# Tying weight sums, and the first addition to h, behind earlier work on VectorE

## The chip, the cores and the metric

One core of a Trainium2 chip runs the whole program. The metric is the device time of one execution in microseconds (us). TensorE (PE) multiplies; its weight loads are a row of their own (PEld). VectorE (DVE), ScalarE (ACT) and GpSimd (POOL) do the elementwise work, and the queue of SyncE (SP) issues nearly all transfers (DMA).

## The reference

A layer of a streaming encoder on x of 512 rows by 1024 columns in float32:

```python
xn = rmsnorm(h, norm_mix_g[l])
u = jnp.einsum('bsd,de->bse', xn, w_in[l])
q, k, v, xr, gr, ga, gb = jnp.split(u, splits, axis=-1)
ya = chunked_band_attention(q, k, v, rel_table[l]) @ w_attn_out[l]
xc = causal_depthwise_conv(xr, conv_w[l], conv_b[l])
hr = rg_lru(xc, w_rg_r[l], b_rg_r[l], w_rg_i[l], b_rg_i[l], rg_lambda[l])
yb = (hr * jax.nn.gelu(gr)) @ w_rnn_out[l]
...
h = h + (g_a * ya + g_b * yb) @ w_o[l]
hn = rmsnorm(h, norm_ffn_g[l])
gu = hn @ w_ffn_in[l]
g, up = jnp.split(gu, 2, axis=-1)
h = h + (jax.nn.silu(g) * up) @ w_ffn_out[l]
```

The change touches three of these products: the v columns of `xn @ w_in`, the product with `w_o` with its addition to h, and `hn @ w_ffn_in`.

## The kernel before

Every float32 operand is held as two parts. `split(hi, lo, src)` writes the high part on ACT (line 82) and then the low part on DVE (line 83), and `mm3` makes each product from three matmuls: high by high (line 76), high by low (line 77), low by high (line 78).

The three products that the change touches are each made by a scheme with seven smaller block products in place of eight. Its kinds have names: `w11`, `w21`, `w22` take a block of the weight as it is, and `t1` to `t4` take sums of blocks: t1 = b12 - b11, t2 = b22 - t1, t3 = t2 - b11, t4 = b21 - t2. One kind is 24 matmuls on PE, and its weights come as two halves, u = 0 and u = 1, each 128 x 2 x 512. For each half a raw block is loaded into a tile `raw` (three of them in turn, and one more in the stage of the ffn), summed if the kind asks for it, and split into a tile `whl` (four in turn, so that two kinds are there at a time).

- Attention stage: `v_weights` (line 272 is the sum for t3, 276 the sum for t4). Kinds in PE's order: w11, t1, t2, w22, t3, w21, t4.
- Stage of w_o: `kept_weights`. Here sums were made ahead and stored in DRAM. `o_add` (line 1193) adds the products `o_x`, `o_y`, `o_z` to the tiles `h`, which are loaded from x by ACT's queue (line 1162). The operands `ms` come from the tiles `za` by the additions of lines 1146 to 1148 and a split.
- Ffn: six units, fg0, fu0, fg1, fu1, fg2, fu2. fg0 takes kept sums (`kept_weights`, its kind t4 loading both parts from DRAM, line 317); the other five are made in `f_weights`: line 350 (`f_sum`) makes t1 and t2, line 366 t3, line 375 t4. Blocks are 512 columns wide, 384 in fg2 and fu2. `gated` (lines 1274, 1281, 1282) adds the products up and gates them; POOL multiplies in part of them.

The order on PE is written out by hand. The order on DVE, ACT and SP in these stages isn't: a planner takes the program as it is written, and at each point gives an engine the ready instruction of highest priority, by a model of when operands are ready. An instruction that comes late in the program can so stand early in its engine's queue. On the chip each queue runs strictly in the order it got. `tc.keep_in_program_order(ins)` ties one instruction: it must stand in its engine's queue behind the one written just before it for that engine. It adds no wait. `weights(name)` makes the weights of the kind asked for and of the next one, so the sums of a kind are written where the product before it begins. In the order of the program that means, on DVE:

- the two sums of t2 are written behind the splits of t1,
- those of t3 behind the splits of w22,
- those of a unit's w11 (they make t1) behind the two additions of `gated(unit, 0, 0, ...)` of the unit before,
- those of v's t3 behind the split of `v_s3`,
- and the first `o_add` behind the splits of the weights of o's t1.

Of the kernel before, what the change touches and what calls it, by code (L numbers as in the profile page):

```python
# [11 lines left out]
ALU = mybir.AluOpType  # L12
# [3 lines left out]
D = 1024  # L16
# [22 lines left out]
def block_kernel(ctx: ExitStack, tc: tile.TileContext, x, norm_mix_g, w_in, b_merge, rel_table,  # L39
# [3 lines left out]
    pe, dve, act, pool, sp = nc.tensor, nc.vector, nc.scalar, nc.gpsimd, nc.sync  # L43
# [24 lines left out]
    def f(ap):  # L68
        return ap.bitcast(F32)
# [10 lines left out]
    def split(hi, lo, src):  # L80

        act.activation(hi, src, AF.Copy)  # L82
        dve.tensor_sub(lo, src, f(hi))  # L83
# [159 lines left out]
    v_t1, v_t2 = [], []  # L243

    def v_raw(kind, kh, half, u):
        raw = wp.tile([P, 2, S], F32, tag="raw", bufs=3, name=f"raw_v_{kind}_{kh}{half}{u}")
        at = kh * S + u * CW
        for n, gr in enumerate(v_groups[half]):
            sp.dma_start(out=raw[:, :, n * CW:(n + 1) * CW],
                         in_=w_in[at:at + CW, C_V + gr * CW:C_V + (gr + 1) * CW].rearrange("(k p) e -> p k e", p=P))  # L250
        return raw[:]
# [10 lines left out]
    def v_weights(kind):  # L262

        hl = [wp.tile([P, 2, 2, S], F32R, tag="whl", bufs=4, name=f"whl_v_{kind}_{u}") for u in range(2)]
        for u in range(2):
            if kind == "t1":
                src = v_t1[u]
            elif kind in ("t2", "t4"):
                src = v_t2[u]
            elif kind == "t3":  # L270
                src = v_raw(kind, 0, 0, u)
                dve.tensor_sub(src, v_t2[u], src)
            else:
                src = v_raw(kind, int(kind[1]) - 1, int(kind[2]) - 1, u)
                if kind == "w21":
                    dve.tensor_sub(v_t2[u], src, v_t2[u])
            split(hl[u][:, 0], hl[u][:, 1], src)
        return lambda part, k: hl[k // 2][:, part, k % 2]

    kept_sums = {(w, n): dr.tile([2, P, D], F32, name=f"{w}_t{n}") for w, n in (("o", 1), ("o", 2), ("f", 1), ("f", 2), ("f", 3))}  # L280
    kept_parts = {(w, n): dr.tile([2, P, 2 * D], F32, name=f"{w}_hl{n}") for w, n in (("o", 3), ("o", 4), ("f", 4))}

    def kept_block(dst, w, kh, half, u):
        at = kh * S + u * CW
        sp.dma_start(out=dst, in_={"o": w_o, "f": w_ffn_in}[w][at:at + CW, half * S:half * S + S].rearrange("(k p) e -> p k e", p=P))
# [24 lines left out]
    def kept_weights(w, kind):  # L310

        if (w, kind) == ("f", "t4"):
            hl = [[sums_room.tile([P, 2, S], F32R, tag=f"t{1 + u}{part}", bufs=1, name=f"whl_f_t4_{u}{part}") for part in range(2)]
                  for u in range(2)]
            for u in range(2):
                for part in range(2):
                    sp.dma_start(out=f(hl[u][part][:]).rearrange("p k e -> p (k e)"), in_=kept_parts[w, 4][u][:, part * D:(part + 1) * D])
            return lambda part, k: hl[k // 2][part][:, k % 2]
        pl, bufs = (o_room[0], 2) if w == "o" and kind in ("w11", "t2", "t4") else (wp, 4)
        hl = [pl.tile([P, 2, 2, S], F32R, tag="whl", bufs=bufs, name=f"whl_{w}_{kind}_{u}") for u in range(2)]  # L320
        for u in range(2):
            if kind[0] == "t" and (w, int(kind[1])) in kept_parts:
                sp.dma_start(out=f(hl[u][:]).rearrange("p a k e -> p (a k e)"), in_=kept_parts[w, int(kind[1])][u])
                continue
            raw = wp.tile([P, 2, S], F32, tag="raw", bufs=3, name=f"raw_{w}_{kind}_{u}")
            if kind[0] == "w":
                kept_block(raw[:], w, int(kind[1]) - 1, int(kind[2]) - 1, u)
            else:
                sp.dma_start(out=raw[:].rearrange("p k e -> p (k e)"), in_=kept_sums[w, int(kind[1])][u])
            split(hl[u][:, 0], hl[u][:, 1], raw[:])  # L330
        return lambda part, k: hl[k // 2][:, part, k % 2]

    f_sums, f_loads, room = {}, [0], []

    def f_side(unit):
        return S if unit[2] != "2" else (DFF - 4 * S) // 2

    def f_raw(unit, kind, kh, side, u):
        wide = f_side(unit)
        f_loads[0] += 1  # L340
        pl, bufs = (room[0], 1) if f_loads[0] % 4 == 0 and room else (wp, 3)
        raw = pl.tile([P, 2, S], F32, tag="raw", bufs=bufs, name=f"raw_{unit}_{kind}_{kh}{side}{u}")
        at, col = kh * S + u * CW, "gu".index(unit[1]) * DFF + int(unit[2]) * 2 * S + side * wide
        sp.dma_start(out=raw[:, :, 0:wide], in_=w_ffn_in[at:at + CW, col:col + wide].rearrange("(k p) e -> p k e", p=P))
        return raw[:, :, 0:wide]

    def f_sum(unit, n, u, a, b):

        t = f_sums[n, u] = sums_room.tile([P, 2, S], F32, tag=f"t{n}{u}", bufs=1, name=f"t{n}_{unit}_{u}")[:, :, 0:f_side(unit)]
        return dve.tensor_sub(t, a, b)  # L350

    def f_weights(unit, kind):

        hl = [wp.tile([P, 2, 2, S], F32R, tag="whl", bufs=4, name=f"whl_{unit}_{kind}_{u}")[:, :, :, 0:f_side(unit)]
              for u in range(2)]
        for u in range(2):
            if kind in ("t1", "t4"):
                src = f_sums[1 if kind == "t1" else 2, u]
            elif kind == "t2":
                ins = f_sum(unit, 2, u, f_raw(unit, kind, 1, 1, u), f_sums[1, u])  # L360
                if u == 0:
                    tc.keep_in_program_order(ins)
                src = f_sums[2, u]
            elif kind == "t3":
                src = f_raw(unit, kind, 0, 0, u)
                ins = dve.tensor_sub(src, f_sums[2, u], src)
                if u == 0:
                    tc.keep_in_program_order(ins)
            else:
                src = f_raw(unit, kind, int(kind[1]) - 1, int(kind[2]) - 1, u)  # L370
            split(hl[u][:, 0], hl[u][:, 1], src)
            if kind == "w11":
                f_sum(unit, 1, u, f_raw(unit, kind, 0, 1, u), src)
            if kind == "w21":
                dve.tensor_sub(f_sums[2, u], src, f_sums[2, u])
        return lambda part, k: hl[k // 2][:, part, k % 2]

    def prefetch(n):
        while len(made) < min(n, len(chunks), index.get(barrier[0], len(chunks))):
            name, parts, rows, kts = chunks[len(made)]  # L380
            if name[:2] == "v_":
                made.append(v_weights(name[2:]))
                continue
            if name[:2] == "o_" or name[:3] == f_units[0]:
                made.append(kept_weights(name[0], name.split("_")[1]))
                continue
            if name[:3] in f_units:
                made.append(f_weights(*name.split("_")))
                continue
# [22 lines left out]
    def weights(name, ahead=1):  # L412
        prefetch(index[name] + 1 + ahead)
        if index[name] + 1 == len(made):
            low_parts()
        return made[index[name]]
# [44 lines left out]
    for n in range(2):  # L461
        pool.dma_start(out=vr[V_BI:V_BI + 8, (1 - n) * 64:(1 - n) * 64 + 64],
                       in_=b_rg_i.rearrange("(t two p) -> two t p", two=2, p=64)[n])
# [725 lines left out]
    def o_add(banks, half, cc, last=False):  # L1189
        for a in range(2):  # L1190
            t = 2 * half + a
            hs = ht[t][:, cc * S:(cc + 1) * S]
            dve.scalar_tensor_tensor(hs, banks[a][:], 0.5, hs, ALU.mult, ALU.add)
            if last:
                junk = tg_.tile([P, S], F32, tag="tg", name=f"hj{t}_{cc}")
                act.activation(junk[:], hs, AF.Square, accum_out=q2[t][:, cc:cc + 1])
# [10 lines left out]
    def o_last_rows(jp):  # L1207
        if jp == 4:
            o_product(ox, "t4", "x22", False)
            o_add(ox, 1, 0, True)  # L1210
            o_rows(1)

    in_order = ExitStack()
    in_order.enter_context(tc.manual_schedule(engines={mybir.EngineType.PE}))
    o_product(ox, "w11", "x11", True)
    o_add(ox, 0, 0)
    o_product(oy, "w21", "x12", True)
    o_add(oy, 0, 0, True)
    o_product(oz, "t1", "s1", True)
    o_add(oz, 1, 1)  # L1220
# [154 lines left out]
    for unit in f_units[1:]:  # L1375
        n, last = int(unit[2]), unit == f_units[-1]
# [120 lines left out]
    def bank(tag, name):  # L1497
        return ps.tile([P, S], F32, tag=tag, bufs=4 if tag == "mm" else 2, name=name)
# [6 lines left out]
    with tc.manual_schedule(engines={mybir.EngineType.PE, mybir.EngineType.DVE}):  # L1505
# [3 lines left out]
        for i in plain:  # L1509
            w = weights(f"fo0_{i}", 3)  # L1510
# [15 lines left out]
        for n, i in enumerate(paired):  # L1526
            w = weights(f"fo0_{i}", 4)
# [20 lines left out]
        for n, i in enumerate(paired):  # L1548
            w = weights(f"t12_{i}", 4)
# [8 lines left out]
        w = weights(f"fo1_{plain[-3]}", 5)  # L1558
# [33 lines left out]
        last = bank("t", "po_last")  # L1592
# [41 lines left out]
```

## Time and profile before

| | us |
|---|---|
| three runs | 860.36, 860.77, 863.06 (median 860.77) |
| the profiled execution's own time | 863.98 |
| its span, first to last instruction | 862.2 |
| PE busy in it | 844.7 |
| DVE busy | 662.3 |
| ACT busy | 519.7 |
| POOL busy | 140.9 |

In lines of the profile, `out<-in` names tiles without their numbers; the first figure of a timeline's row is the start in us from the span's start, the second its length in us, and what stands in brackets is the idle time of the engine just before it and what ended that. A row of waits gives the sum, the number and the longest. PEclk is the granted share of PE's clock.

### The profile page before, as it was taken

What the parts mean: (1) busy time and instruction counts of PE and PEld (TensorE: products, weight loads), DVE (VectorE), ACT (ScalarE), POOL (GpSimd) and SP (SyncE); (2) the same over time, 40 slices, a digit from 0 to 9 for tenths busy, and PEclk for the clock granted to TensorE, in tenths of its full rate; (3) what the DMA queues carried; (4) which work ended last, traced back from release to release, by engine and by line L of the source; (5) the groups of instructions that cost most, each with busy time, mean ns of one, the idle gap of its engine ahead of it and who ended that gap; (6) DMA issues with size and microseconds to landing.
All of it is one profiled execution on the core that took longest, in us unless ns stands there. A gap on an engine that the chain in (4) does not pass through costs nothing.

```text
span 862.2 us, 11589 instructions
## 1 busy us (share of the span) xinstructions
PE 844.7 (98%) x4114; PEld 712.7 (83%) x4114; DVE 662.3 (77%) x972; ACT 519.7 (60%) x864; POOL 140.9 (16%) x179
## 2 busy tenths in 40 slices
PE   9999999999989999999999999999999999999996
PEld 7988888888868888888888787888878999988885
DVE  5667869886979788887568577788678777798985
ACT  7595848763356688787544458653664565655434
POOL 2402031231030133333000000014002212200000
PEclk9999999999999999999999999999999999999999
DMA  8433487675634333222234873545454444426642
GB/s 284 161 114 106 149 284 268 201 265 201 203 114 146 111 98 97 89 75 73 74 110 133 326 280 129 189 153 170 145 172 137 122 141 144 166 87 200 215 135 97
DMA packets 95385, 137.17 MB, mean 159 GB/s; under 512 B 7288, under 2 KB 62160, under 8 KB 94816
## 3 DMA queue, kind: packets, MB, share of 16 engines
q1 hardware_dynamic: 93696, 132.93, 47.3%
q10 hardware_dynamic: 1232, 2.95, 0.9%
q8 instruction: 32, 0.52, 0.3%
q0 software_dynamic: 400, 0.57, 0.2%
q14 instruction: 25, 0.20, 0.1%
HBM read 122.75 MB, written 13.67 MB: 158 GB/s over the span
## 4 chain that ended last, share of the span: by engine, by line
PE 68%; DVE 13%; DMA 11%; ACT 4%; issue 4%; DVEq 0%; ACTq 0%; SPq 0%
DMA raw_fu_w<-in_w_ffn_in_dram 3%; PE po_out L76 2%; PE po_out L77 2%; PE po_out L78 2%; PE o L1084 2%; PE pT L1064 2%; DMA raw_fg_w<-in_w_ffn_in_dram 2%; PE po_ga L78 2%; PE po_ya L76 2%; PE po_ya L77 2%; PE po_ya L78 2%; PE po_ga L76 2%; PE po_ga L77 2%; DMA raw_fu_t<-in_w_ffn_in_dram 1%; PE po_xr L77 1%
## 5 line engine op out<-in xcount | busy, mean ns | idle before, releaser
L1282 POOL TENSOR_TENSOR sg<-sg,keep_fu_x 128x512 f32<-128x512 f32 (+1 forms) x10 | 18.3, 1853 | 240.4 <-DVE keep_fu_x L1281 240.4
L1053 POOL TENSOR_SCALAR p<-p,rl 128x128 f32<-128x128 f32 (+3 forms) x61 | 42.7, 718 | 15.6 <-DVE rl L1049 14.8
L1047 DVE CUSTOM_DVE_ANT_0 p<-s,bias 128x128 f32<-128x128 f32 (+1 forms) x64 | 28.6, 485 | 11.1 <-PE s L1039 8.2
L1048 ACT ACTIVATE p<-p,m 128x128 f32<-128x128 f32 (+1 forms) x64 | 35.5, 555 | 2.5 <-DVE m L1047 2.2
L76 PE MATMUL po_out<-whl_fo,act_hi 128*128 128x512 f32 (+1 forms) x80 | 30.9, 386 | 0.0
L78 PE MATMUL po_out<-whl_fo,act_lo 128*128 128x512 f32 (+1 forms) x80 | 30.7, 384 | 0.0
L77 PE MATMUL po_out<-whl_fo,act_hi 128*128 128x512 f32 (+1 forms) x80 | 30.7, 384 | 0.0
L83 DVE TENSOR_TENSOR pp<-pT,pp 128x384 fp32r<-128x384 f32 (+1 forms) x48 | 26.9, 595 | 2.0 <-ACT pp L82 1.8
L77 PE MATMUL po_xr<-xnT,whl_xr 128*128 128x512 f32 (+1 forms) x80 | 27.7, 353 | 0.0
L77 PE MATMUL po_gr<-xnT,whl_gr 128*128 128x512 f32 (+1 forms) x80 | 27.5, 347 | 0.0
L78 PE MATMUL po_gr<-xnT,whl_gr 128*128 128x512 f32 (+1 forms) x80 | 27.3, 347 | 0.0
L78 PE MATMUL po_xr<-xnT,whl_xr 128*128 128x512 f32 (+1 forms) x80 | 27.2, 346 | 0.0
L76 PE MATMUL po_gr<-xnT,whl_gr 128*128 128x512 f32 (+1 forms) x80 | 27.1, 347 | 0.0
L83 DVE TENSOR_TENSOR whl_fo<-raw_fo,whl_fo 128x1024 fp32r<-128x1024 f32 x16 | 20.7, 1303 | 8.0 <-ACT whl_fo L82 8.0
L76 PE MATMUL po_xr<-xnT,whl_xr 128*128 128x512 f32 (+1 forms) x80 | 26.3, 351 | 0.4 <-ACT xnT L611 0.4
L82 ACT ACTIVATE whl_fu_t<-t_fu 128x1024 fp32r<-128x1024 f32 (+1 forms) x18 | 17.6, 985 | 13.0 <-PE fu_x L78 8.7
L76 PE MATMUL po_k<-xnT,whl_qk 128*128 128x512 f32 x64 | 25.5, 398 | 0.0
L76 PE MATMUL po_q<-xnT,whl_qk 128*128 128x512 f32 x64 | 25.5, 398 | 0.0
L76 PE MATMUL po_ga<-xnT,whl_ga 128*128 128x512 f32 x64 | 25.5, 398 | 0.0
L1275 ACT ACTIVATE sg<-sg 128x512 f32<-128x512 f32 (+1 forms) x20 | 11.9, 596 | 22.4 <-DVE sg L1274 22.0
L76 PE MATMUL po_gb<-xnT,whl_gb 128*128 128x512 f32 x64 | 25.2, 394 | 0.0
L78 PE MATMUL po_ga<-xnT,whl_ga 128*128 128x512 f32 x64 | 25.0, 391 | 0.1
(614 smaller groups left out, 3003.3 us busy)
## 6 DMA issues: line engine op xcount, KB each, us to landing
raw_qk<-in_w_in_dram SPq DMA_DIRECT2D x32, 256.0 KB, 3.1
raw_fu_w<-in_w_ffn_in_dram SPq DMA_DIRECT2D x16, 512.0 KB, 4.3
raw_fo<-in_w_ffn_out_dram SPq DMA_DIRECT2D x16, 512.0 KB, 4.1
raw_xr<-in_w_in_dram SPq DMA_DIRECT2D x8, 512.0 KB, 5.7
raw_gr<-in_w_in_dram SPq DMA_DIRECT2D x8, 512.0 KB, 4.7
raw_ga<-in_w_in_dram SPq DMA_DIRECT2D x8, 512.0 KB, 3.9
raw_gb<-in_w_in_dram SPq DMA_DIRECT2D x8, 512.0 KB, 3.8
o_b<-in_w_o_dram SPq DMA_DIRECT2D x8, 512.0 KB, 6.3
```

The lines of the kernel that those rows point to most:

```text
L76: pe.matmul(o, sh, mh, start=start, stop=False, skip_group_check=parts)
L77: pe.matmul(o, sh, ml, start=False, stop=False, skip_group_check=parts)
L78: pe.matmul(o, sl, mh, start=False, stop=stop, skip_group_check=parts)
L82: act.activation(hi, src, AF.Copy)
L83: dve.tensor_sub(lo, src, f(hi))
L1047: dve.tensor_tensor_reduce(prob[qb][:], scs[qb][:, 0:w], bias[:, S - w:S], -1.0, 3e38, ALU.add, ALU.min, nmax[:, qb:qb + 1])
L1048: act.activation(prob[qb][:], prob[qb][:], AF.Exp, bias=nmax[:, qb:qb + 1], scale=-1.0, accum_out=lsum[:, qb:qb + 1])
L1053: eng.tensor_scalar(prob[qb][:], prob[qb][:], rl[:, qb:qb + 1], 1.0, ALU.mult, ALU.mult)
L1064: pe.transpose(pt[:, at * P:(at + 1) * P], prob[qb][:, kb * P:(kb + 1) * P], ident[:])
L1084: pe.matmul(po[:, S - n:S], st, pp[i][:, part, lo:lo + n], start=kb == 0 and part == 0, stop=kb == NT - 1 and part == 1)
L1275: ins = act.activation(o, o if keep else banks[a], AF.Silu)
L1282: (pool if keep and (unit != f_units[-1] or side) else dve).tensor_mul(o, o, keep[a] if keep else banks[a])
```

## The change

It ties more of the sums, and moves two lines of the program; no instruction is added or removed.

- v's t3: both sums are tied (none was).
- kind w11 of an ffn unit: both sums (for t1) are tied and written ahead of the split of the same half (they were untied and written behind it).
- kinds t2 and t3: both sums are tied (only u = 0 was), and both are written ahead of the two splits.
- w21: the sum for t4 is written ahead of the split, untied as before.
- fg0's t4: the first of its four loads of stored parts is tied on SP.
- the first addition to h is tied on DVE.

```diff
@@ v_weights
             elif kind == "t3":
                 src = v_raw(kind, 0, 0, u)
-                dve.tensor_sub(src, v_t2[u], src)
+                tc.keep_in_program_order(dve.tensor_sub(src, v_t2[u], src))
@@ kept_weights
             for u in range(2):
                 for part in range(2):
-                    sp.dma_start(out=..., in_=kept_parts[w, 4][u][:, part * D:(part + 1) * D])
+                    ins = sp.dma_start(out=..., in_=kept_parts[w, 4][u][:, part * D:(part + 1) * D])
+                    if u == part == 0:
+                        tc.keep_in_program_order(ins)
@@ f_weights
+        srcs = []
         for u in range(2):
             if kind in ("t1", "t4"):
                 src = f_sums[1 if kind == "t1" else 2, u]
             elif kind == "t2":
-                ins = f_sum(unit, 2, u, f_raw(unit, kind, 1, 1, u), f_sums[1, u])
-                if u == 0:
-                    tc.keep_in_program_order(ins)
+                tc.keep_in_program_order(f_sum(unit, 2, u, f_raw(unit, kind, 1, 1, u), f_sums[1, u]))
                 src = f_sums[2, u]
             elif kind == "t3":
                 src = f_raw(unit, kind, 0, 0, u)
-                ins = dve.tensor_sub(src, f_sums[2, u], src)
-                if u == 0:
-                    tc.keep_in_program_order(ins)
+                tc.keep_in_program_order(dve.tensor_sub(src, f_sums[2, u], src))
             else:
                 src = f_raw(unit, kind, int(kind[1]) - 1, int(kind[2]) - 1, u)
-            split(hl[u][:, 0], hl[u][:, 1], src)
             if kind == "w11":
-                f_sum(unit, 1, u, f_raw(unit, kind, 0, 1, u), src)
+                tc.keep_in_program_order(f_sum(unit, 1, u, f_raw(unit, kind, 0, 1, u), src))
             if kind == "w21":
                 dve.tensor_sub(f_sums[2, u], src, f_sums[2, u])
+            if kind in ("w11", "w21"):
+                split(hl[u][:, 0], hl[u][:, 1], src)
+            else:
+                srcs.append(src)
+        for u, src in enumerate(srcs):
+            split(hl[u][:, 0], hl[u][:, 1], src)
@@ o_add
-            dve.scalar_tensor_tensor(hs, banks[a][:], 0.5, hs, ALU.mult, ALU.add)
+            ins = dve.scalar_tensor_tensor(hs, banks[a][:], 0.5, hs, ALU.mult, ALU.add)
+            if half == a == cc == 0 and not last:
+                tc.keep_in_program_order(ins)
```

More of the change, by code (lines that the diff above doesn't have):

```diff
@@ L316, in kept_weights @@
                 for part in range(2):
-                    sp.dma_start(out=f(hl[u][part][:]).rearrange("p k e -> p (k e)"), in_=kept_parts[w, 4][u][:, part * D:(part + 1) * D])
+                    ins = sp.dma_start(out=f(hl[u][part][:]).rearrange("p k e -> p (k e)"), in_=kept_parts[w, 4][u][:, part * D:(part + 1) * D])
+                    if u == part == 0:
+                        tc.keep_in_program_order(ins)
             return lambda part, k: hl[k // 2][part][:, k % 2]
```

## The prediction, as made before the run

> **What bounds the kernel now.** I read the page's busy times and chain first, then PE's list of waits, then the clock by windows, then the timelines of DVE, ACT and SP around each wait.
>
> ```profile
> PE 844.7 (98%) x4114; PEld 712.7 (83%) x4114; DVE 662.3 (77%) x972; ACT 519.7 (60%) x864; POOL 140.9 (16%) x179
> PE 68%; DVE 13%; DMA 11%; ACT 4%; issue 4%; DVEq 0%; ACTq 0%; SPq 0%
> ```
>
> PE is busy 98% of the span (844.7 us), so an order on DVE can bring only what PE loses. The chain still spends 24% on DVE and DMA: there are stretches in which PE runs on weights that arrive just in time. Where they came late, PE's waits say:
>
> ```profile
> PE v_z L77 <- DVE whl_v_t L83: 3.5, 1, 3.5
> PE o_z L78 <- DVE ms L83: 1.9, 1, 1.9
> PE fu_x L77 <- DVE whl_fu_t L83: 1.6, 1, 1.6
> PE fg_x L77 <- DVE whl_fg_t L83: 1.3, 2, 0.7
> PE fg_y L77 <- DVE whl_fg_w L83: 0.4, 1, 0.4
> ```
>
> Each ends with a low part (line 83) written by DVE. They sum to 8.7 us, and two cost more than their length, as the windows show (busy times, then PEclk, DMA share, GB/s):
>
> ```profile
> 249.33:252.74 3.41, 0.54 (x2) 0.49 (x3) 3.14 (x4) 0.56 (x1) 3.29 (x3) 1.00 0.01 2
> 252.74:256.15 3.41, 3.41 (x9) 2.63 (x8) 3.31 (x4) 3.38 (x5) 0.00 (x0) 0.50 0.00 0
> 484.85:488.26 3.41, 1.55 (x7) 0.87 (x6) 3.41 (x6) 1.21 (x3) 0.00 (x0) 1.00 0.94 354
> 488.26:491.67 3.41, 3.41 (x9) 2.65 (x9) 0.97 (x2) 3.03 (x5) 0.00 (x0) 0.50 0.55 211
> 720.32:723.74 3.42, 2.33 (x13) 2.33 (x14) 3.42 (x5) 0.64 (x2) 0.00 (x0) 1.00 0.13 17
> ```
>
> After a window in which PE was busy 0.54 or 1.55 of 3.41 us, it runs 3.41 us at half clock: 3.41 x 0.5 = 1.71 us lost each time. After 2.33 us busy nothing follows. The Trainium skill ("TensorE: Matmul & The Clock Gate", Part 1) puts the fall of the clock behind an idle window of about 3.4 us. By that rule the second stall, of 1.9 us, would have cost no clock and the sum below would be 1.71 less; the trace shows that it did, and the sum goes by the trace.
>
> **Part 1: v's t3.** The timelines of ACT, DVE and PE show:
>
> ```profile
> 243.82 1.99 ACT L82 ACTIVATE whl_v_t<-v_t 128x1024 fp32r<-128x1024 f32 x2
> 245.86 0.16 DVE L1049 RECIPROCAL rl<-l 128x4 f32<-128x4 f32 x1
> 249.60 1.41 DVE L272 TENSOR_TENSOR raw_v_t<-v_t,raw_v_t 128x1024 f32<-128x1024 f32 x1 [3.58 <-DMA raw_v_t<-in_w_in_dram]
> 250.93 1.21 DVE L83 TENSOR_TENSOR whl_v_t<-v_t,whl_v_t 128x1024 fp32r<-128x1024 f32 x1
> 260.24 1.22 DVE L83 TENSOR_TENSOR v_s3l<-v_s,v_s3h 128x1024 fp32r<-128x1024 f32 x1
> 263.44 1.06 ACT L82 ACTIVATE whl_v_t<-raw_v_t 128x1024 fp32r<-128x1024 f32 x1 [0.76 <-PE v_x L78]
> 252.20 0.50 PE L77 MATMUL v_z<-whl_v_t,v_s1h 128*128 128x512 f32 x1 [3.53 <-DVE whl_v_t L83]
> ```
>
> A sum for t3, two kinds early, stands at the head of DVE's queue and waits 3.58 us for its block. Behind it stands the low part of t1, whose high part was done at 245.81. Without the sum it runs from 246.02 to 247.23; PE wants it at 252.20 - 3.53 = 248.67. So the stall goes whole: 3.53, and with it the slow window, 1.71. The sum's new place is behind v_s3l (260.24), where its block has long landed. It makes the block good for the split of 263.44 and frees no buffer, so being later delays no load: cost 0, hidden as long as it ends by 263.44 (1.98 us after 261.46, for one sum of 1.41). If not, the excess falls on a split with a whole product in hand. Gain 5.24.
>
> **Part 2: the first addition to h, and the load on SP.** One row of the chain, then the timelines of DVE, PE and SP:
>
> ```profile
> 472.73 7.88 DMA h<-in_x_dram
> 480.70 0.69 DVE L1193 SCALAR_TENSOR_TENSOR h<-o_x,h 128x512 f32<-128x512 f32 x1 [4.81 <-PE o_y L77]
> 481.31 0.41 DVE L1146 TENSOR_TENSOR za<-za,za 128x256 f32<-128x256 f32 x1
> 481.64 1.22 DVE L83 TENSOR_TENSOR whl_o_t<-raw_o_t,whl_o_t 128x1024 fp32r<-128x1024 f32 x1
> 482.78 0.42 DVE L1147 TENSOR_TENSOR za<-za,za 128x256 f32<-128x256 f32 x1
> 487.99 0.59 PE L78 MATMUL o_z<-whl_o_t,ms 128*128 128x512 f32 x1 [1.86 <-DVE ms L83]
> 471.36 0.32 SPq L317 DMA_DIRECT2D whl_f_t<-f_hl  x1
> 504.80 0.38 SPq L285 DMA_DIRECT2D raw_f_w<-in_w_ffn_in_dram  x1
> ```
>
> DVE's row names PE, but the addition began when the load of h had landed (472.73 + 7.88 = 480.61): a load is what DVE waits 4.81 us for. Tied, the addition stands behind the low part of 481.64, so at least L1146 and that low part run during the wait. They took 482.78 - 481.31 = 1.47 us: the low end, with 1.86 - 1.47 = 0.39 of the stall left. If L1147 and its successor pass too, all 1.86 goes; that is the high end. I take 1.86 less 0.2, nearer the high end, because L1147 comes earlier in the program. Either way a window of 3.41 has at least 3.41 - 0.39 = 3.02 busy, above the 2.33 that cost nothing, so 1.71 goes as well. Queued behind the addition are then the other low parts of w_o's weights, used a product later.
>
> The tie on SP moves one load of 0.5 MB from 471.36 to behind 504.80. It is wanted by fg0's third product, 25 us later. At the 354 GB/s of the window above, 0.5 MB takes 1.5 us, so h lands up to 1.5 earlier. If the three others stay where they are, perhaps nothing. Ends 0 and 1.5; I take 0, since the stall is already gone. A cost below nothing would come only by contention with loads at 506, with 20 us in hand.
>
> **Part 3: the ffn's sums.** DVE's timeline, with one row of POOL's:
>
> ```profile
> 631.27 1.23 DVE L350 TENSOR_TENSOR t_fu<-raw_fu_w,raw_fu_w 128x1024 f32<-128x1024 f32 x1 [0.89 <-DMA raw_fu_w<-in_w_ffn_in_dram]
> 632.42 1.22 DVE L83 TENSOR_TENSOR whl_fg_t<-t_fg,whl_fg_t 128x1024 fp32r<-128x1024 f32 x1
> 697.84 0.96 DVE L350 TENSOR_TENSOR t_fu<-raw_fu_w,raw_fu_w 128x768 f32<-128x768 f32 x1 [0.51 <-DMA raw_fu_w<-in_w_ffn_in_dram]
> 698.16 2.89 POOL L1371 TENSOR_TENSOR act_lo<-act,act_hi 128x1024 fp32r<-128x1024 f32 x1 [22.17 <-ACT act_hi L1370]
> 698.71 3.15 DVE L83 TENSOR_TENSOR whl_fg_w<-raw_fg_w,whl_fg_w 128x768 fp32r<-128x768 f32 x1
> 705.13 0.96 DVE L350 TENSOR_TENSOR t_fu<-raw_fu_w,raw_fu_w 128x768 f32<-128x768 f32 x1 [0.51 <-DMA raw_fu_w<-in_w_ffn_in_dram]
> 718.53 1.96 DVE L366 TENSOR_TENSOR raw_fu_t<-t_fu,raw_fu_t 128x768 f32<-128x768 f32 x1 [1.35 <-DMA raw_fu_t<-in_w_ffn_in_dram]
> 720.41 0.94 DVE L83 TENSOR_TENSOR whl_fu_t<-t_fu,whl_fu_t 128x768 fp32r<-128x768 f32 x1
> ```
>
> All four of PE's ffn stalls have one pattern: a sum for a later kind waits for its block (0.89, 0.51, 0.51, 1.35) and the low part that PE wants stands behind it. Each sum takes 1 to 2 us besides its wait, more than the stall it makes (0.7, 0.4, 0.6, 1.6). At 698.71 the low part without the sum starts near 697.3 and misses the POOL instruction that stretched it. Tied, the L350 sums stand behind the additions of `gated(0, 0)`, after t4's low parts; L366 behind w22's. So all of 3.4 goes.
>
> What it costs: a unit's w11 sums now wait for the additions at the end of the unit before. Take fu0 to fg1, in the timelines of POOL, DVE and PE and a row of the chain:
>
> ```profile
> 592.05 4.45 POOL L1282 TENSOR_TENSOR sg<-sg,keep_fu_x 128x512 f32<-128x512 f32 x2 [1.76 <-DVE keep_fu_x L1281]
> 593.62 1.71 DVE L83 TENSOR_TENSOR whl_fg_w<-raw_fg_w,whl_fg_w 128x1024 fp32r<-128x1024 f32 x1
> 595.02 0.39 PE L76 MATMUL fg_x<-whl_fg_w,hn 128*128 128x512 f32 x1
> 595.25 0.39 PE L77 MATMUL fg_x<-whl_fg_w,hn 128*128 128x512 f32 x1
> 593.13 4.08 DMA raw_fg_t<-in_w_ffn_in_dram
> ```
>
> Matmuls start 595.25 - 595.02 = 0.23 apart, so a product is 24 x 0.227 = 5.45, and t4 before it began at 589.57: the additions can end at about 589.57 + 0.2 (the last matmul's 0.39 beyond the step of 0.23) + 0.69 (the addition of 480.70, of the same shape) = 590.5. Sum, low part, sum, low part, at some 1.15 each, end at 595.1. PE wants the first low part at 595.25 (it is there at 592.8) and the second at the eighth matmul, 595.02 + 7 x 0.227 = 596.61: 1.5 in hand. One multiplication of line 1282 between costs 0.7. Beside POOL's multiplications a DVE operation took 1.71 in place of 1.2, 0.5 more; two of them cost 1.0. So at worst by rows 0.2 is missed, at each of two passages from a u unit to a g unit; 0 to 0.4 together, and I take 0.2. At the passages from g to u POOL does nothing. The next loads start when these blocks are freed, at 595.1 in place of 593.13: landed at 599.2 (4.08 later). Their two sums and two low parts, 4.6 us, end by 603.8. t2 starts two products after 595.02, at 605.9 or later: 2.1 in hand, cost 0. The sums of t2 and t3 ahead of both splits, and t4's sum ahead of w21's, put one sum (1.15) more before a low part that has some 2 in hand as well: cost 0, and 0.1 a kind if that cover goes.
>
> **The sum.** 3.53 + 1.71 + 1.86 + 1.71 + 3.4 = 12.2, less 0.2 for part 2, 0.2 for part 3, and 0.2 for a new small wait = 11.6. Against the profiled execution's 863.98: 852.4. The runs' median, 860.77, is 3.2 lower. The three runs are 860.36, 860.77 and 863.06; the step of 2.3 is near one slow window (1.71). A stall of 1.86 lies over half in one window of 3.41 only in some runs, so I take the median to lack the second slow window: 11.6 - 1.71 = 9.9, and 860.77 - 9.9 = 850.9.
>
> **The rivals.**
>
> 1. POOL takes back a part. The w11 sums now start just when POOL multiplies what the additions gave. The low part of 698.71 took 3.15 beside POOL's instruction of 698.16, where that of 720.41 took 0.94; it was held to about the other's end, which speaks for it. 1.71 for 1.2 at 593.62 speaks against. As a mechanism from rows: at each of two passages two operations are held by 2.2 (half of 4.45), and 4.4 less the 1.5 in hand is 2.9, twice: 850.9 + 5.8 = 856.7; 854 to 858.2 as a case, 0.18. The Trainium skill ("SBUF — State Buffer", the section on two separate sides) says of a DVE operation with two SBUF inputs and a GpSimd one that whichever starts first gets the shared ports for the whole instruction, the other "fully blocks". By that rule this rival's time is the forecast; 698.71 agrees with it, 593.62 does not.
> 2. The change does not do what it says: the planner, whose order shifts elsewhere, brings other sums or loads ahead of needed low parts. Only sums are tied; L375 is not, nor three of the loads on SP. Against it: PE's list holds no other wait over 0.4 us but that at the very start. Gains of 9.9 given back to within the bound: 858.2 to 863.4, middle 860.8. 0.11.
> 3. Slower: blocks freed late. With three or four raw tiles, a tied sum that holds its block holds the next load, and each of five ffn units falls behind. It decides from 9.9 / 5 = 2.0 lost in each unit, with 2.1 in hand: a delay of 4.1 a unit, one more round of a load (4.08). At 5 x 2.8 lost: 865. Against it: DVE has 98 - 77 = 21 points of the span less to do than PE. 0.09.
>
> **How the numbers follow.** Forecast 0.57: 848.1 to 854. Better, 0.05: second slow window in the median after all. About 0.3%, 2.6 us, is what a measurement here can tell from no change. Faster 0.57 + 0.05 + 0.18 = 0.80, same 0.11, slower 0.09. The low end 848.1 is all 12.2 with 0.5 for runs; the high end 859.5 takes in rival 1 and the near half of rival 2.
>
> **What would show it.** Right: PE's waits on whl_v_t and ms are gone, no window at half clock in the middle, no wait of L272 or L350 ahead of a low part in need. Part 2's low end: a wait on ms of about 0.4. Rival 1: PE waits at the second low part of w11 in fg1 and fg2. Rival 3: DVE waits on DMA at L350 for t2, with PE's waits on t2 in every unit. The prediction is wrong if PE's idle time stays near 10 us.

## The result, and the profile after

| | before | after | ratio, 95% interval |
|---|---|---|---|
| median, us | 861.91 (860.36 to 863.39, 4 runs) | 849.93 (849.69 to 850.82, 4 runs) | 0.9863 (0.984 to 0.9886) |
| profiled execution, us | 863.98, span 862.2 | 849.69, span 847.9 | |

The change makes the kernel 12.0 us faster by the medians, 14.3 by the two profiled spans. From the page of the changed kernel, its busy times and chain:

```profile
PE 839.1 (99%) x4114; PEld 710.8 (84%) x4114; DVE 663.2 (78%) x972; ACT 522.5 (62%) x864; POOL 140.6 (17%) x179
PE 82%; DVE 8%; ACT 4%; DMA 3%; issue 2%; ACTq 0%; DVEq 0%
```

The work is the same: the counts of these five engines are those of before. PE's share of the chain rose from 68 to 82%, and DMA's fell from 11 to 3%: PE runs on weights that arrive just in time in far less of the span. PE's listed waits are now these three, all in the first 25 us:

```profile
PE busy L439 <- DVE eps_t L445: 1.2, 1, 1.2
PE po_xr L76 <- ACT xnT L615: 0.4, 2, 0.2
PE pt_mix_0t L613 <- DVE xs_mix L593: 0.2, 1, 0.2
```

All five lines shown of before are gone, and so are the two windows at half clock. Two windows at the places of the two long stalls (busy times of PE, PEld, DVE, ACT, POOL, then PEclk, DMA share, GB/s):

```profile
248.41:251.82 3.41, 3.31 (x15) 2.43 (x14) 3.38 (x3) 2.98 (x5) 3.41 (x2) 1.00 0.00 0
480.00:483.41 3.41, 3.41 (x16) 2.83 (x16) 1.68 (x3) 2.57 (x4) 0.00 (x0) 1.00 0.90 330
```

DVE's timeline at v (lines of the source stand 2 to 6 further down than before):

```profile
244.51 0.16 DVE L1053 RECIPROCAL rl<-l 128x4 f32<-128x4 f32 x1
244.59 1.19 DVE L83 TENSOR_TENSOR whl_v_t<-v_t,whl_v_t 128x1024 fp32r<-128x1024 f32 x1
254.54 1.21 DVE L83 TENSOR_TENSOR v_s3l<-v_s,v_s3h 128x1024 fp32r<-128x1024 f32 x1
255.68 1.21 DVE L272 TENSOR_TENSOR raw_v_t<-v_t,raw_v_t 128x1024 f32<-128x1024 f32 x1
```

The low part of t1 follows the reciprocal at once; the sum that waited 3.58 us for its block now runs behind v_s3l, with no wait. The stall isn't gone to the last bit, though, as ACT, DVE and PE show:

```profile
245.82 1.06 ACT L82 ACTIVATE v_s4h<-v_s 128x1024 fp32r<-128x1024 f32 x1 [2.30 <-DVE whl_v_t L83]
247.86 1.42 DVE L83 TENSOR_TENSOR whl_v_t<-v_t,whl_v_t 128x1024 fp32r<-128x1024 f32 x1 [1.48 <-ACT whl_v_t L82]
249.33 0.50 PE L77 MATMUL v_z<-whl_v_t,v_s1h 128*128 128x512 f32 x1
```

Before, ACT made both high parts of t1 together (243.82, two instructions). Now the split of v_s4 stands between them in its queue and waits 2.30 us, so the second low part of t1 ends only at 247.86 + 1.42 = 249.28. PE, which issues a matmul every 0.23 us here, issued the one before at 248.84 and the one that reads this part at 249.33. With the longer step behind it that is 0.4 us, too little for the list of waits.

At o, DVE's and SP's timelines:

```profile
470.54 0.42 DVE L1151 TENSOR_TENSOR za<-za,za 128x256 f32<-128x256 f32 x1
470.89 1.22 DVE L83 TENSOR_TENSOR whl_o_t<-raw_o_t,whl_o_t 128x1024 fp32r<-128x1024 f32 x1
473.49 0.69 DVE L1197 SCALAR_TENSOR_TENSOR h<-o_x,h 128x512 f32<-128x512 f32 x1 [1.39 <-DMA h<-in_x_dram]
473.46 2.60 SPq L285 DMA_DIRECT2D raw_o_w<-in_w_o_dram  x2
```

The second sum for ms (L1147 before, L1151 now) and the low part run ahead of the first addition to h, whose wait for its load fell from 4.81 to 1.39 us. The passage from fu0 to fg1, on DVE, POOL and PE:

```profile
579.10 1.30 POOL L1288 TENSOR_TENSOR sg<-sg,keep_fu_x 128x512 f32<-128x512 f32 x1
579.76 1.72 DVE L83 TENSOR_TENSOR whl_fg_w<-raw_fg_w,whl_fg_w 128x1024 fp32r<-128x1024 f32 x1 [1.17 <-ACT whl_fg_w L82]
581.40 1.21 DVE L352 TENSOR_TENSOR t_fg<-raw_fg_w,raw_fg_w 128x1024 f32<-128x1024 f32 x1
582.54 0.68 DVE L1287 TENSOR_TENSOR keep_fu_x<-fu_y,keep_fu_x 128x512 f32<-128x512 f32 x1
583.14 1.21 DVE L352 TENSOR_TENSOR t_fg<-raw_fg_w,raw_fg_w 128x1024 f32<-128x1024 f32 x1
583.29 2.21 POOL L1288 TENSOR_TENSOR sg<-sg,keep_fu_x 128x512 f32<-128x512 f32 x1 [2.90 <-DVE keep_fu_x L1287]
584.27 2.31 DVE L83 TENSOR_TENSOR whl_fg_w<-raw_fg_w,whl_fg_w 128x1024 fp32r<-128x1024 f32 x1
585.27 0.39 PE L76 MATMUL fg_x<-whl_fg_w,hn 128*128 128x512 f32 x1
```

PE begins w11 at 585.27 and wants its second low part at the eighth matmul, 585.27 + 7 x 0.227 = 586.86. The low part ends at 584.27 + 2.31 = 586.58. So 0.3 us is in hand, and no more.

**Where 14.3 us came from.** A stall costs PE more than its listed idle: the step to the stalled matmul is longer than the usual step by the idle plus 0.16 (the modelled length of the matmul before it, 0.39, less the step of 0.23), and the step after it is 0.11 longer. That is 0.27 beside every listed wait (rows under e6). A window at half clock cost less than the 1.71 that the prediction takes, as PE's timeline of before shows:

```profile
253.22 0.63 PE L77 MATMUL v_z<-whl_v_t,v_s1h 128*128 128x512 f32 x1
253.65 0.63 PE L78 MATMUL v_z<-whl_v_t,v_s1l 128*128 128x512 f32 x1
259.16 0.39 PE L76 MATMUL v_x<-whl_v_t,v_s2h 128*128 128x512 f32 x1
```

A step at half clock is 0.43, not quite twice 0.227. From the stalled matmul of 252.20 to that of 259.16, 23 steps later, it is 6.96 us in place of 23 x 0.227 = 5.22. Of the 1.74 too much, 0.11 is the step behind the stall, so the window cost 1.6; the one at o cost 1.6 too, counted in the same way.

In the trace of before: v_z 3.53 + 0.27 = 3.80; o_z 1.86 + 0.27 = 2.13; four waits in the ffn 3.4 + 4 x 0.27 = 4.5; two windows at half clock, 3.2. Together 13.6, less the 0.4 that is left at v: 13.2. By the matmuls' starts PE in the trace of before falls another 0.9 us behind ahead of v's stall, at a wait of 0.25 (`s L1038 <- DVE m L1047`) and at smaller steps. That part isn't the change's: the profiles of e3 and e11, without v's tie, lack this wait, and that of e5, with it, has it. With it the sum is 14.1 of the 14.3.

### The profile page after: what moved, and what is told of

Its sections match the earlier page's. It is cut to its first block, busy times and chain, and to the rows that moved or that the text cites. A ratio compares the mean times of both kernels' runs of the same rounds, so it can differ in the third digit from the quotient of the medians.

```text
span 847.9 us, 11598 instructions
## 1 busy us (share of the span) xinstructions
PE 839.1 (99%) x4114; PEld 710.8 (84%) x4114; DVE 663.2 (78%) x972; ACT 522.5 (62%) x864; POOL 140.6 (17%) x179
## 4 chain that ended last, share of the span: by engine, by line
PE 82%; DVE 8%; ACT 4%; DMA 3%; issue 2%; ACTq 0%; DVEq 0%
PE fu_x L78 2%; PE fu_x L76 2%; PE fu_x L77 2%; PE po_out L76 2%; PE po_out L77 2%; PE po_out L78 2%; PE o L1088 2%; PE fg_x L78 2%; PE fg_x L76 2%; PE fg_x L77 2%; PE pT L1068 2%; PE po_ga L78 2%; PE po_ya L78 2%; PE po_ya L77 2%; PE po_ya L76 2%
## 5 line engine op out<-in xcount | busy, mean ns | idle before, releaser
L1051 DVE CUSTOM_DVE_ANT_0 p<-s,bias 128x128 f32<-128x128 f32 (+1 forms) x64 | 28.6, 485 | 11.6 <-PE s L1043 10.2
L83 DVE TENSOR_TENSOR whl_fu_w<-raw_fu_w,whl_fu_w 128x1024 fp32r<-128x1024 f32 (+1 forms) x18 | 22.1, 1227 | 8.5 <-ACT whl_fu_w L82 8.5
L83 DVE TENSOR_TENSOR whl_fu_t<-t_fu,whl_fu_t 128x1024 fp32r<-128x1024 f32 (+1 forms) x18 | 23.8, 1324 | 4.8 <-ACT whl_fu_t L82 4.6
L82 ACT ACTIVATE whl_fu_w<-raw_fu_w 128x1024 fp32r<-128x1024 f32 (+1 forms) x18 | 17.8, 989 | 13.0 <-issue 7.1
L76 PE MATMUL po_ga<-xnT,whl_ga 128*128 128x512 f32 x64 | 25.4, 397 | 0.0
```

Of the source, the lines that this page charges most:

```text
L76: pe.matmul(o, sh, mh, start=start, stop=False, skip_group_check=parts)
L1051: dve.tensor_tensor_reduce(prob[qb][:], scs[qb][:, 0:w], bias[:, S - w:S], -1.0, 3e38, ALU.add, ALU.min, nmax[:, qb:qb + 1])
```

## The experiments

Kernels e1 to e4 were timed beside runs of the kernel before with a median of 861.79 (23 runs); e5, e6, e10, e11 beside 862.31 (7); e7, e8, e9 beside 862.47 (7). Ratios are to these.

**e1, e4, e2, e3: each part alone, on the kernel before.**

e1, v's tie:

```diff
-                dve.tensor_sub(src, v_t2[u], src)
+                tc.keep_in_program_order(dve.tensor_sub(src, v_t2[u], src))
```

> The kernel before with the two sums of v's t3 tied, nothing else. Theory A (each tie takes away one stall of its own, and a stall costs PE its listed idle time, some 0.27 us around it and, where it fell, a slow window): PE's wait on whl_v_t goes (3.53), with 0.14 around it and 1.7 of half clock, so 5.4 us less, ratio 0.9937; o_z and the ffn keep their waits (1.9, 3.4 in sum). Theory B (PE, once ahead, meets the next late operand): PE's waits behind the v stage grow by what was gained, and the time falls by under 2.5 us.

856.41 us, 0.9945 (0.9928 to 0.9962): theory A. The wait of v_z is gone. The wait of o_z was shorter in this profile, 1.5 us, with this window around it:

```profile
478.41:481.82 3.41, 1.91 (x9) 1.28 (x8) 3.41 (x6) 1.06 (x3) 0.00 (x0) 1.00 1.03 410
```

No window at half clock follows: with 1.5 idle, any window of 3.41 has at least 1.9 busy.

e4, the tie on SP:

```diff
+                    if u == part == 0:
+                        tc.keep_in_program_order(ins)
```

> The kernel before with only the first load of fg0's t4 tied on SP. Theory A: no stall of PE hangs on it; 0 us, the wait on ms stays at 1.9. Theory B (the load held up the queue and the load of h): h lands 1.5 us or more earlier, the wait on ms falls to 0.4 or less and the second slow window goes: 1.5 to 3.5 us less.

861.0 us, 0.9989 (0.9975 to 1.0004): no difference that this can tell. o_z still waits, 1.1 us; it waited 1.1 in e3's profile too, which hasn't this tie, so the smaller wait is no effect of it.

e2, the tie on the first addition to h:

```diff
+            if half == a == cc == 0 and not last:
+                tc.keep_in_program_order(ins)
```

> The kernel before with only the first addition to h tied. Theory A: it runs behind one low part and L1146 to L1147 and the wait on ms is 0 to 0.4 us; 2.0 us less, and 3.7 less against those runs of before that had a second slow window. Theory B: the addition still waits for the load of h at the head of the queue and the wait on ms stays above 1 us; under 1 us less.

861.2 us, 0.9994 (0.9975 to 1.0014). The wait on ms is gone, yet the median is only 0.6 us lower. The interval reaches to 2.1 us less, so theory A's 2.0 is at its very edge. PE's waits and DVE's timeline in the ffn say where the gain went:

```profile
PE fg_x L77 <- DVE whl_fg_t L83: 2.2, 3, 1.2
PE s L1038 <- DVE m L1047: 0.7, 1, 0.7
629.79 1.23 DVE L350 TENSOR_TENSOR t_fu<-raw_fu_w,raw_fu_w 128x1024 f32<-128x1024 f32 x1 [1.10 <-DMA raw_fu_w<-in_w_ffn_in_dram]
632.20 0.50 PE L77 MATMUL fg_x<-whl_fg_t,hn 128*128 128x512 f32 x1 [1.20 <-DVE whl_fg_t L83]
```

fg_x waited 1.3 us in all before, 2.2 now. The untied sum stands ahead of the low part and waits for a load; PE comes earlier, the load not by as much, so part of the gain is given back there. The starts of the same matmuls in the two traces give the size. PE in e2 is 0.5 us behind before at the matmul ahead of o_z's stall (486.19 for 485.73), 3.3 ahead of it once the stall and the window at half clock are past (488.45 for 491.74), and 1.5 ahead at fu2's stall (719.93 for 721.41): 3.8 gained, 1.8 given back. Against an execution of before without the second window at half clock the gain at o would be 2.1, by the stall's steps, and 1.8 given back leaves little of that. (The wait of 0.7 on m lies ahead of all that this edit touches.)

e3, the sums of the ffn as changed (f_weights whole, of which this is the core):

```diff
+                tc.keep_in_program_order(dve.tensor_sub(src, f_sums[2, u], src))
...
+                tc.keep_in_program_order(f_sum(unit, 1, u, f_raw(unit, kind, 0, 1, u), src))
...
+        for u, src in enumerate(srcs):
+            split(hl[u][:, 0], hl[u][:, 1], src)
```

> The kernel before with f_weights as changed (ties on both sums of t1, t2 and t3, sums ahead of the splits), nothing else. Theory A: PE's four waits in the ffn go, 3.39 idle and 0.27 around each: 4.5 us less, ratio 0.9948. Theory B: PE comes to the ffn no earlier than before and the late part only moves: under 2 us less, with a wait of PE on the second low part of w11 in fg1 or fg2.

856.93 us, 0.9945 (0.9924 to 0.9965), as theory A has it. One wait of 0.5 is left in the ffn. The profile holds v's stall at 3.5 us as before, but more of the clock is lost behind it:

```profile
246.89:250.30 3.41, 0.87 (x4) 0.38 (x2) 1.67 (x2) 0.00 (x0) 2.88 (x5) 1.00 0.21 74
250.30:253.71 3.41, 2.50 (x6) 2.02 (x7) 3.31 (x4) 2.50 (x3) 1.33 (x1) 0.50 0.00 0
253.71:257.13 3.42, 3.42 (x10) 2.65 (x9) 2.79 (x3) 2.13 (x4) 0.00 (x0) 0.50 0.00 0
```

Two windows at half clock in place of one. The first of them begins while PE still stands (it starts again at 251.21), so it costs less than a whole one: from 251.21 to the 23rd step behind it, at 259.33, it is 8.12 us, 2.9 too much, where before has 1.74. The same stall so costs one window or two, here 1.2 us more.

The four ratios leave 4.7 + 0.9 + 0.5 + 4.7 = 10.8 us; the change brings 11.8.

**e11: the tie on h with the sums of the ffn** (the edits of e2 and e3), to see whether e2's gain comes out once the ffn gives nothing back.

```diff
+            if half == a == cc == 0 and not last:
+                tc.keep_in_program_order(ins)
...
+                tc.keep_in_program_order(f_sum(unit, 1, u, f_raw(unit, kind, 0, 1, u), src))
...
```

> The kernel before with the tie on the first addition to h and with the sums of the ffn as in the changed kernel; v's sum and SP's load stay as before. Alone, the tie on h took the wait on ms away and left the time (0.9994), and the ffn's ties alone gave 0.9945. Theory A (what the h tie gained was given back at the untied sums of the ffn, whose waits for blocks go by the loads and not by PE): with both, no wait on ms and no wait of the ffn, the time is 1.4 to 2.2 us less than with the ffn's ties alone, ratio 0.992 to 0.993 to the kernel before. Theory B (the wait on ms costs no time at all, because PE catches up behind it on something else): the same as the ffn's ties alone, ratio 0.9945.

854.59 us, 0.9905 (0.989 to 0.9919), clear of e3's interval. PE's only long wait is v's 3.5. The step from e3 is 3.4 us by the ratios, more than the 1.4 to 2.2 expected. This profile lost one window behind v and e3's two: v_z's 24 matmuls took 10.79 us here (247.70 to 258.49) and 11.96 in e3's (247.37 to 259.33), which is 1.2 of it, if the other runs were alike. So the tie on h is worth about 2 us beside the ffn's ties; alone, no gain of it shows clear of the noise.

**e6: the change without the tie on h.**

```diff
-            ins = dve.scalar_tensor_tensor(hs, banks[a][:], 0.5, hs, ALU.mult, ALU.add)
-            if half == a == cc == 0 and not last:
-                tc.keep_in_program_order(ins)
+            dve.scalar_tensor_tensor(hs, banks[a][:], 0.5, hs, ALU.mult, ALU.add)
```

> The changed kernel without the tie on the first addition to h; the tie on SP stays. Theory A (the addition stands again ahead of the first sums for ms and waits for h's load): PE has a wait on ms of 1.1 to 1.9 us, as in the kernels that had the other ties alone, and the time is 1.4 to 2.2 us (the wait and 0.27 beside it) above the changed kernel, 3.9 with a window at half clock behind it: ratio 0.988 to 0.991 to the kernel before. Theory B (the load on SP alone brings h in time, or what is gained at ms is given back later): no wait on ms, or one that does not show in the time, ratio 0.986.

852.34 us, 0.9879 (0.9864 to 0.9893): theory A, at its lower edge. DVE's and PE's timelines:

```profile
474.95 0.69 DVE L1197 SCALAR_TENSOR_TENSOR h<-o_x,h 128x512 f32<-128x512 f32 x1 [4.09 <-DMA h<-in_x_dram]
480.41 0.39 PE L76 MATMUL o_z<-whl_o_t,ms 128*128 128x512 f32 x1
480.64 0.39 PE L77 MATMUL o_z<-whl_o_t,ms 128*128 128x512 f32 x1
482.24 0.50 PE L78 MATMUL o_z<-whl_o_t,ms 128*128 128x512 f32 x1 [1.21 <-DVE ms L83]
482.58 0.40 PE L76 MATMUL o_z<-whl_o_t,ms 128*128 128x512 f32 x1
```

With the tie on SP kept, the addition still waits 4.09 us and PE 1.21. These rows also price a stall: the step to the stalled matmul is 1.60, less the usual 0.23 makes 1.37, and the next step of 0.34 adds 0.11. That is 1.48 for a listed 1.21.

**e5: the change without the tie on SP.**

```diff
-                    if u == part == 0:
-                        tc.keep_in_program_order(ins)
```

> The changed kernel without the tie on SP's load: the first of the four loads of f_hl is again issued early, as in the kernel before. Theory A (the tie on SP brings nothing by itself, because the wait on ms went with the tie on DVE, and PE has slack there): PE has no wait on ms over 0.2 us, h lands up to 1.4 us later than in the changed kernel, and the time is that of the changed kernel, ratio 0.986 (0.984 to 0.988) to the kernel before. Theory B (the tie is needed, since h's load and the raw weights of w_o share SP's queue with it): the raw_o_w loads again issue some 9 us later, behind a wait of SP on h of about 7 us, DVE waits for them in the next product and PE has a wait of over 1 us near 480 to 495, ratio 0.988 or more.

849.74 us, 0.9854 (0.9839 to 0.9868): theory A. SP's timeline of e5:

```profile
468.11 6.86 SPq L317 DMA_DIRECT2D whl_f_t<-f_hl  x3
475.07 2.23 SPq L285 DMA_DIRECT2D raw_o_w<-in_w_o_dram  x2
```

SP is held 6.86 us at these loads, but the weights of w_o are issued only 1.6 later than in the changed kernel, not 9, and PE has no wait there. So theory B fails already in its premise.

**e9: the change without the tie on w11's sums.**

```diff
-                tc.keep_in_program_order(f_sum(unit, 1, u, f_raw(unit, kind, 0, 1, u), src))
+                f_sum(unit, 1, u, f_raw(unit, kind, 0, 1, u), src)
```

> The changed kernel without the tie on w11's sums; those of t2 and t3 stay tied, and the new order inside the kinds stays. Theory A (the sums of w11 waiting for their blocks made three of the four waits of the ffn, 0.4 to 0.7 us each): PE has two or three waits of 0.3 to 0.9 us on whl_fg_t or whl_fg_w again, with 0.27 beside each the time is 1.5 to 3 us above the changed kernel, ratio 0.988 to 0.990. Theory B (w11's ties are needless once those of t2 and t3 hold the order): no wait, ratio 0.986, and DVE has the sums of w11 earlier, out of POOL's way.

852.05 us, 0.9887 (0.985 to 0.9925): theory A. The old pattern is back, with the waits shown here:

```profile
694.76 0.96 DVE L352 TENSOR_TENSOR t_fu<-raw_fu_w,raw_fu_w 128x768 f32<-128x768 f32 x1 [0.73 <-DMA raw_fu_w<-in_w_ffn_in_dram]
695.64 0.95 DVE L83 TENSOR_TENSOR whl_fg_t<-t_fg,whl_fg_t 128x768 fp32r<-128x768 f32 x1
696.65 0.44 PE L77 MATMUL fg_x<-whl_fg_t,hn 128*128 128x384 f32 x1 [0.85 <-DVE whl_fg_t L83]
```

A second wait, of 0.88 at fg_y, follows a low part that POOL's instruction stretched to 3.16. With 0.17 at fu2 the three cost 1.9 + 3 x 0.27 = 2.7; the median is 2.1 above the changed kernel's. The interval takes in that kernel's 0.9863, so it is the waits that decide here, and not the time.

**e8: the change with each split at its old place**, the ties kept.

```diff
+            split(hl[u][:, 0], hl[u][:, 1], src)
             if kind == "w11":
...
-            if kind in ("w11", "w21"):
-                split(hl[u][:, 0], hl[u][:, 1], src)
-            else:
-                srcs.append(src)
-        for u, src in enumerate(srcs):
-            split(hl[u][:, 0], hl[u][:, 1], src)
```

> The changed kernel with the ties, but with each split of f_weights at its old place in the loop: in w11 the sum is issued after its split, and of t2 and t3 the second sum stands after the first split. Theory A (only the ties matter; the order of a sum and a split inside a kind hides behind PE): the changed kernel's time, ratio 0.986 (0.984 to 0.988), no PE wait in the ffn over 0.3 us. Theory B (the new order inside the kinds is needed too): the sum of the second half waits behind the first split at t2 and t3, ACT gets its source 1.1 us later, and PE waits 0.3 to 1 us at some of the ten kinds, ratio 0.988 to 0.992.

853.91 us, 0.991 (0.9878 to 0.9942): theory B, with two waits of 1.8 and 1.5 us at t3 of fu0 and of fu2. Its timelines of DVE, ACT and PE at the first, and then the changed kernel's rows for the same two second halves:

```profile
565.31 1.23 DVE L373 TENSOR_TENSOR t_fu<-raw_fu_w,t_fu 128x1024 f32<-128x1024 f32 x1 [1.99 <-DMA raw_fu_w<-in_w_ffn_in_dram]
567.59 1.22 DVE L366 TENSOR_TENSOR raw_fu_t<-t_fu,raw_fu_t 128x1024 f32<-128x1024 f32 x1
568.90 1.06 ACT L82 ACTIVATE whl_fu_t<-raw_fu_t 128x1024 fp32r<-128x1024 f32 x1 [3.92 <-DVE raw_fu_t L366]
570.46 2.30 DVE L83 TENSOR_TENSOR whl_fu_t<-raw_fu_t,whl_fu_t 128x1024 fp32r<-128x1024 f32 x1
572.82 0.50 PE L77 MATMUL fu_x<-whl_fu_t,bts 128*128 128x512 f32 x1 [1.78 <-DVE whl_fu_t L83]
```

```profile
560.99 2.35 DVE L367 TENSOR_TENSOR raw_fu_t<-t_fu,raw_fu_t 128x1024 f32<-128x1024 f32 x2
564.20 1.05 ACT L82 ACTIVATE whl_fu_t<-raw_fu_t 128x1024 fp32r<-128x1024 f32 x1
566.67 1.22 DVE L83 TENSOR_TENSOR whl_fu_t<-raw_fu_t,whl_fu_t 128x1024 fp32r<-128x1024 f32 x1
```

Tied behind the first low part, the second sum of t3 comes after w21's sum (untied), which waits 1.99 us for its block. ACT gets its source 4.7 us later (568.90 for 564.20), and the low part meets POOL. Both sums ahead of the splits is a part of the gain, not a neutral move: about 4 us here.

**e10: POOL's gating multiplications of fu0 and fu1 done twice**, the first time into a scratch tile, so that the real product comes later as well.

```diff
+                if keep and unit != f_units[-1]:
+                    again = tg_.tile([P, S], F32, tag="tg", name=f"again_{unit}_{half}{side}{a}")
+                    pool.tensor_mul(again[:, 0:f_side(unit)], o, keep[a])
```

> The changed kernel with every multiplication of POOL in the gating of fu0 and fu1 done a second time into a scratch tile that nobody reads: POOL works twice as long there, the order on the other engines is that of the changed kernel. Theory lock (a VectorE operation beside a POOL operation waits for POOL's end and then runs its 1.1 us; the passage from u to g has 0.3 us in hand): the two sums and two low parts of w11 in fg1 and fg2 are held by 1.2 to 2.2 us more at each passage, so that PE waits for the second low part (whl_fg_w) of fg1 and of fg2 by 0.9 to 1.9 us each; with 0.27 beside each listed wait the time is 2.3 to 4.3 us above the changed kernel, ratio 0.989 to 0.991 to the kernel before. Theory share (the two only slow each other, 0.5 us for a VectorE operation, as the row of 593.62 was read in the prediction): 0.5 to 1.0 later, PE waits of 0.2 to 0.7, ratio 0.987 or less; with no wait at all POOL does not matter there.

854.05 us, 0.9903 (0.9887 to 0.992): theory lock in time, and at fg1 in place:

```profile
584.47 2.28 POOL L1291 TENSOR_TENSOR sg<-sg,keep_fu_z 128x512 f32<-128x512 f32 x1
585.52 2.32 DVE L83 TENSOR_TENSOR whl_fg_w<-raw_fg_w,whl_fg_w 128x1024 fp32r<-128x1024 f32 x1
587.89 0.50 PE L77 MATMUL fg_x<-whl_fg_w,hn 128*128 128x512 f32 x1 [1.01 <-DVE whl_fg_w L83]
```

POOL ends at 586.75, the low part 1.09 later, and PE waits 1.01 for it. At fg2 the expected wait did not come. Another, of 1.02 on ACT (pt_act, 676.68), stands near it, and POOL is behind that one too: DVE's two sums of t2 (L352, from 671.19) took 4.01 us beside POOL, ACT waited 4.23 us for them, and the copy that PE needed stood behind that in ACT's queue.

**e7: these multiplications on VectorE.** The edit takes all 16 of POOL's gating multiplications, four of them fu2's, which the expectation counts to fu0 and fu1.

```diff
-                (pool if keep and (unit != f_units[-1] or side) else dve).tensor_mul(o, o, keep[a] if keep else banks[a])
+                dve.tensor_mul(o, o, keep[a] if keep else banks[a])
```

> The changed kernel with the gating multiplications of fu0 and fu1 on VectorE in place of POOL: 16 more DVE operations of about 0.7 us, none of POOL there. Theory A (POOL holds DVE at the passage from u to g for 0.5 to 1.2 us a time, so POOL's work costs DVE as much as doing it itself): the low parts of w11 come no later, 0.3 us in hand or more, no new PE wait, ratio 0.986. Theory B (DVE has no room for 2 x 0.7 us more at the passage, where 0.3 us is in hand): PE waits of 0.4 to 1.1 us at fg1 and fg2, ratio 0.988 to 0.989.

851.82 us, 0.9883 (0.9851 to 0.9915). Theory B's waits at fg1 and fg2 are not there, as theory A says; the second low part of fg1 runs in its bare length:

```profile
583.81 1.22 DVE L83 TENSOR_TENSOR whl_fg_w<-raw_fg_w,whl_fg_w 128x1024 fp32r<-128x1024 f32 x1
707.25 4.02 DVE L83 TENSOR_TENSOR whl_fu_w<-raw_fu_w,whl_fu_w 128x768 fp32r<-128x768 f32 x2
```

But at 707.25 two low parts of fu2 wait for another instruction of POOL (3.12 us, begun at 706.47), and 0.6 us of PE is lost at t3 there. The profile also has a wait of 0.5 at v_z, ahead of anything this edit touches, as e5 and e6 have: it is the one behind the split of v_s4, 0.8 us with its steps in place of the changed kernel's 0.4. Of the 2.2 us that this profile is longer than the changed kernel's (by the matmuls' starts), 1.1 lies ahead of the edit, so the time confirms neither A nor B.

## Why the prediction was right, and where its terms were off

The median came 1.0 us under the 850.9 forecast, inside the likeliest case. Its steps:

- **Part 1, 5.24.** Right in place and mechanism: e1 alone gave 4.7, no stall and no half clock. By the trace of before it was 3.80 + 1.6. "The stall goes whole" is too much: 0.4 is left at t1's second low part (0.8 in e5, e6 and e7). The prediction looked at the first low part alone, and took ACT's order as it was. (e1 has the new order on ACT and no delay: DVE came to this place 1.5 us earlier there.)
- **Part 2, 1.86 + 1.71 less 0.2.** Right on the high end: L1151 and the low part pass the addition and no wait on ms is left, so the 0.2 was not due. The load on SP, valued at 0, is worth nothing that shows (e4, e5). What the step missed is that the gain hangs on part 3: alone it gave 0.5 by the ratio (e2, with an interval from a loss of 1.2 to a gain of 2.1), beside it about 2 (e11, and e6 against e5: 2.6 by medians, 2.2 by ratios). That the ffn gave it back is seen in e2's trace; the two times alone would not prove it.
- **Part 3, 3.4.** All four waits went (e3; in e9 two of them come back). Two steps inside it fell short. First, both sums ahead of the splits were weighed as a cost, of 0. That cost is 0, but the order is needed: e8 shows that with the old lines the tied sum of t3 makes waits of 1.8 and 1.5. Second, the order at the passage from u to g was another. The forecast had addition, sum, low part, sum, low part, with 1.5 in hand. In fact u = 1's sum, tied behind u = 0's low part, ran ahead of the second addition, u = 0's sum behind it, and the second low part last (read from the rows and the ties): 0.3 in hand.
- **Rival 1, POOL.** Right as a mechanism, without a price here. The row at 593.62 was misread: POOL's row at 592.05 groups two instructions, 4.45 together, so the first ended near 592.05 + 2.22 = 594.27, and 594.27 + 1.08 is 595.35, where the DVE operation ended (593.62 + 1.71 = 595.33). It was held to POOL's end like that of 698.71. In the changed kernel 579.10 + 1.30 + 1.08 = 581.48 = 579.76 + 1.72, and 583.29 + 2.21 + 1.08 = 586.58 = 584.27 + 2.31. The Trainium skill ("SBUF — State Buffer", the section on two separate sides) says that the one which starts first holds the shared ports for its whole instruction; the rows of this passage agree. It cost nothing because the hold ended 0.3 us early, and e10 shows the cost from there on.
- **Rivals 2 and 3.** No wait of L375 (now L373) or of t2's sums reaches PE. Rival 2 is there in small: with v's tie the planner also put the split of v_s4 between the two high parts of t1 on ACT, for the 0.4 above.
- **The sum.** 11.6 was too little against the profiled execution. 6 x 0.27 = 1.6 for the six stalls is missing, since the list of waits was taken as PE's loss; this is the term that was mis-sized. The 0.2 each for parts 2 and 3 were not due, the new small wait cost 0.4 in place of 0.2, and the two windows 0.1 each less than 1.71: 11.6 + 1.6 + 0.4 - 0.2 - 0.2 = 13.2. The rest of the measured 14.3 is for the most part the 0.9 ahead of v, which differs from run to run.
- **The median.** That it lacks a part of the clock loss was right in kind: 14.3 by the profiled runs, 12.0 by medians. The later median of before, 861.91, is 1.1 above the 860.77 used. So a gain 2.1 too small and a base 1.1 too low made the 1.0: two misses that partly cancel, and that much of the closeness is luck. The reason given, that the stall lies over half in one window only in some runs, is not shown. In the other profiles that keep this stall it was shorter (1.5 in e1, 1.1 in e3 and e4, 1.2 in e6) and no window at half clock followed, so most runs may just have had a shorter stall.

## What to carry to other kernels

When a planner puts an instruction that waits for a load ahead of a ready one, look at what is queued behind it: the wait is paid by the next engine, and a gain upstream can be paid back at the next such place, so tie them all before judging one. When sums are tied, check what the tie places ahead of them, too. And read a stall from the starts of the matmuls around it, not from the listed idle alone.

## What the runs showed of the hardware

- A stall of PE cost about 0.27 us beside its listed idle: 1.48 for 1.21 in e6, and, by the starts of the same matmuls in two traces, 2.1 for 1.8 in e8 and 1.1 for 0.85 in e9.
- The granted clock changed only at multiples of 3.41 us from one another within a run. It fell to half after windows with 0.54 and 1.55 of 3.41 us busy (before) and 0.87 (e3), and not after one with 1.79 (e4, 715.86 to 719.27) or 1.59 (e1, 846.05 to 849.46); the ends of matmuls are modelled, so these bounds are rough. The Trainium skill ("TensorE: Matmul & The Clock Gate", Part 1) names an idle window of about 3.4 us; 1.86 us of idle was enough in the trace of before.
- It came back after one window at half clock that was 3.41 busy (before) or 3.28 (e11, 251.49 to 254.90), and not after one of 2.50 (e3). So v's stall of 3.5 us was followed by one such window or by two, 1.6 or 2.8 us, as its end lay to the windows. A matmul's step was 0.43 us at half clock and 0.227 at full.
- Such windows go with a part of the scatter. One of them is 0.002 of the mean granted clock. Over 37 runs of the kernel before that clock lay between 0.994 and 0.999, the times between 857.86 and 865.94, and the two have a correlation of -0.64. It isn't all: e1's six runs, all at 0.998 or 0.999, still differ by 2.7 us. The changed kernel's four, at the same clocks, lie within 1.2 us.
- A DVE operation of 128 x 1024 with both inputs in SBUF that began beside a running one of POOL ended 1.08 us after POOL's end, at each such place of the passage from fu0 to fg1, and one of 128 x 768 0.81 after it (698.16 + 2.89 + 0.81 = 698.71 + 3.15, before). An addition with one input in PSUM was not held: in the changed kernel that of L1287 at 572.69 took its usual 0.68 beside POOL's 2.14 from 571.78.
